# First FFN of a diffusion layer: the up projection by seven block products instead of eight, weight sums by accumulating transfers, hidden tiles through DRAM and the down projection as a phase of its own

## The chip, the core and the metric

The kernel runs on one core of one Trainium2 chip, in one launch. The core has a matrix engine (PE, with its weight loads shown as PEld), a vector engine (DVE), a scalar engine (ACT), GpSimd (POOL) and a queue engine (SP) that issues most DMAs. Times are device microseconds (us) of a whole execution; a version's time is the median of its runs. The profile comes from one execution and names instructions by line of the kernel (L118 is line 118).

## The reference, cut to what matters

One layer (DEPTH = 1) of a diffusion backbone on two sequences of 256 tokens, context and latent, with D = 2048. It begins with a half-step FFN on both sequences, with shared weights; then come a mixer (attention beside an mLSTM), a second FFN on the latent tokens alone and a last norm. All is f32.

```
def half_step_ffn(x, mod, i, g, w_up, w_down):
    h = adaln(x, g, mod, i)
    a, b = jnp.split(h @ w_up, 2, axis=-1)
    return x + 0.5 * mod[:, i + 2, None, :] * ((jax.nn.silu(a) * b) @ w_down)
...
xl = half_step_ffn(xl, mod_l, 0, g_norm[l, 0], w_ffn1_up[l], w_ffn1_down[l])
xc = half_step_ffn(xc, mod_c, 0, g_norm[l, 0], w_ffn1_up[l], w_ffn1_down[l])
```

`mod` has nine rows per sequence: `silu(c) @ w_mod + b_mod` (w_mod is 2048 x 18432). The hidden width D_FF is 5632, 44 columns of 128 (NF), 11 blocks of 512 (FB = 4 columns, CB = 512). `w_up` gives both halves a and b.

## The kernel before

**Products.** Every f32 operand is split into a part that the float32r format holds (`hi`, copied by ACT, L101) and the rest (`lo`, subtracted by DVE, L102). `mm3` (L116) then makes three matmuls, hi x hi, hi x lo, lo x hi (L118 to L120). Activations are split once and stay in SBUF (`hhi`, `hlo`, 512 tokens, context and latent side by side). Weights come from DRAM in tiles of 128 x 2048 f32 (1 MB): `load_split` (L111) issues the load on SP into one of three `raw` buffers, and `split` (L93) makes two halves of 1024 columns, each with its own `hi` and `lo` (four buffers each, so two weight tiles). A tile's halves come free when PE has read them.

**First FFN.** The prologue computes modulation rows 0 and 1 and the norm, and starts the first three columns (NPRE) in six PSUM banks. `ffn` with nt = 4 (L280 on) then goes through the 44 columns: `up` (L302) loads the two halves a and b of a column, with weights stationary and 512 tokens moving: 16 x 3 matmuls each. `tail` (L282) makes silu (L286), gating (L287) and the split of the hidden tile (L298, L299); the tile lies with its columns on partitions, as the down projection needs it. After every fourth column `down` (L367) runs the block before: four column blocks of the output, four token tiles, 4 x 3 matmuls each with 512 weight columns moving, added to `acc` by DVE (L378; the first block is copied by ACT, L376). The last block is `last1` (L508), where the residual, the norm of the next sub-layer and its transposes are woven in. The residual's rows x are added to `acc` by a DMA with accumulation that POOL issues (L506), four in all.

**Modulation rows 2 to 8** are a side job of this FFN: `mod_steps` (L183) loads 224 half tiles of 512 KB (`sraw`, three buffers) and DVE multiplies each with the conditions `cB` and sums (L168, `mod_half`): one product for rows 5 to 8 (latent alone), two for rows 2 to 4, 320 in all. After every `load_split` of the FFN `next(side)` lets a few go; `due` counts products, and MOD_PACE = 3 sets how many.

**Order.** The framework writes each engine's queue: among the instructions whose inputs it takes to be ready, the one earliest in the program goes first, and a buffer's reuse waits for its last reader. `keep_in_program_order` puts an instruction behind the one traced before it on its engine; later ones may still go ahead of it. Each engine then runs its own queue strictly in order.

**Second FFN** (nt = 2): here the weights move (512 columns), tokens are stationary, 24 matmuls for each 1 MB tile; the gated tiles are turned by PE transposes (L359) and copied by ACT (L362).

Of the kernel before, what the change touches and what calls it, by code (L numbers as in the profile page):

```python
# [18 lines left out]
P = 128  # L19
# [11 lines left out]
MOD_PACE = 3.0  # L31
# [17 lines left out]
def tile_layer(ctx: ExitStack, tc: tile.TileContext, I: dict, out: bass.AP):  # L49
# [22 lines left out]
    tri_f = cst.tile([P, P], F32, name="tri_f")  # L72
    tri_b = cst.tile([P, P], F32, name="tri_b")
# [4 lines left out]
    nc.gpsimd.affine_select(out=tri_f, in_=ones, pattern=[[1, P]], compare_op=ALU.is_ge, fill=0.0, base=0, channel_multiplier=-1)  # L78
    nc.gpsimd.affine_select(out=tri_b, in_=ones, pattern=[[-1, P]], compare_op=ALU.is_ge, fill=0.0, base=0, channel_multiplier=1)
    nc.vector.tensor_tensor(ident, tri_f, tri_b, op=ALU.mult)  # L80
# [35 lines left out]
    def mm3(out_ap, sh, sl, mh, ml, first, last):  # L116

        nc.tensor.matmul(out_ap, sh, mh, start=first, stop=False)  # L118
        nc.tensor.matmul(out_ap, sh, ml, start=False, stop=False)  # L119
        nc.tensor.matmul(out_ap, sl, mh, start=False, stop=last)  # L120
# [8 lines left out]
    def sumsq(dst, x, n=512):  # L129
        junk = sm.tile([P, 1024], BF16, tag="junk", name="junk", bufs=1)  # L130
        nc.scalar.activation(junk[:, :n], x, AF.Square, accum_out=dst)
# [25 lines left out]
    mod_rows = {i: dr.tile([2, D], F32, name=f"mod{i}") for i in (2, 5, 8)}  # L157

    cbcm = pool(name="cb", bufs=1)
    cbp = cbcm.__enter__()  # L160
    cB = cbp.tile([P, 2, D], F32, name="cB")
    mT = cbp.tile([P, 9, 2, KT, 2], F32, name="mT")

    def mod_half(raw, i, seqs, kt, h, pinned=False):

        for s in seqs:
            junk = sm.tile([P, 1024], BF16, tag="junk", name="junk", bufs=1)
            ins = nc.vector.scalar_tensor_tensor(  # L168
                junk, raw, 1.0, cB[:, s, h * 1024 : (h + 1) * 1024], op0=ALU.mult, op1=ALU.mult, accum_out=mT[:, i, s, kt, h : h + 1]
            )  # L170
            if pinned:
                tc.keep_in_program_order(ins)
# [10 lines left out]
    def mod_steps(sp):  # L183

        due = 0.0
        for i in range(2, 9):
            seqs = (CTX, LAT) if i < 5 else (LAT,)
            for kt in range(KT):
                for h in range(2):
                    raw = sp.tile([P, 1024], F32, tag="sraw", name="sraw", bufs=3)  # L190
                    nc.sync.dma_start(raw, I["w_mt"][i - 2, kt, :, h * 1024 : (h + 1) * 1024])
                    mod_half(raw, i, seqs, kt, h, True)
                    due += len(seqs)
                    while due > 0:
                        due -= MOD_PACE
                        yield
            for s in seqs:
                n, q = divmod(i, 3)
                if q < 2:
                    dst = (SH, SC)[q][:, n, s, :]  # L200
                    mod_sum(dst, i, s, slice(0, KT))
                    if q:
                        scale_of(n, s, slice(0, KT))
                    continue
                v = sm.tile([P, KT], F32, tag="gv", name="gv")
                mod_sum(v, i, s, slice(0, KT))
                pg = tbank()
                nc.tensor.transpose(pg[:KT, :P], v, ident)
                gr = sm.tile([KT, P], F32, tag="gr", name="gr")
                nc.vector.tensor_copy(gr, pg[:KT, :P])  # L210
                nc.sync.dma_start(mod_rows[i][s, :].rearrange("(k p) -> k p", p=P), gr)
# [5 lines left out]


# [11 lines left out]
    def affine_split(src, n, s, k0, hh, hl):  # L230

        h = sm.tile([P, 2, 256], F32, tag="h", name="h")
# [14 lines left out]
    def drain(it):  # L247
        for _ in it:
            pass
# [29 lines left out]
    def ffn(wup, wdn, hhi, hlo, nt, hp, acc, residual, last, side=iter(()), started=(), row=None):  # L279
        N = nt * P  # L280

        def tail(pab, row=None, dst=None):  # L282
# [14 lines left out]
            hh, hl = dst or [hp.tile([P, N], F32R, tag=g, name=g, bufs=5) for g in ("hidh", "hidl")]  # L297
            nc.scalar.activation(hh, sa, AF.Copy)  # L298
            nc.vector.tensor_tensor(hl, sa, hh.bitcast(F32), op=ALU.subtract)  # L299
            return hh, hl  # L300

        def up(f, dst=None):  # L302
            pab = []
            for ab in range(2):
                wt = load_split(wup[f, ab])
                next(side, None)
# [5 lines left out]
            return tail(pab, None, dst)  # L312
# [54 lines left out]
        def down(n, hids, acc_first, final, between=iter(())):  # L367

            for cb in range(NCB):
                wt = load_split(wdn[n, cb])  # L370
                next(side, None)
# [12 lines left out]
        if nt == 2:  # L384
            hids = []
            for f in range(FB):
                hh, hl = pair() if f % 2 == 0 else (hh, hl)
                dst = hh[:, f % 2, :], hl[:, f % 2, :]
                hids.append(tail(started[f], row, dst) if f < len(started) else up(f, dst))
            for n in range(1, NF // FB):  # L390
                nxt = []
                sab = gated(up_block(n))
                down(n - 1, hids, n == 1, n == NF // FB - 1, turned(sab, nxt))
                hids = nxt
            last(lambda wt, t: block(hids, wt, t))
            return
        hid = {}
        for f in range(NF):
            hid[f] = tail(started[f], row) if f < len(started) else up(f)
            if f % FB == 0 and f:  # L400
                down(f // FB - 1, [hid.pop(q) for q in range(f - FB, f)], f == FB, f // FB == NF // FB - 1)
        hids = [hid.pop(q) for q in range(NF - FB, NF)]
# [8 lines left out]
    hhi = hpool.tile([P, KT, 512], F32R, name="hhi")  # L411
    hlo = hpool.tile([P, KT, 512], F32R, name="hlo")

    pre = [[bank(), bank()] for _ in range(NPRE)]
    with pool(name="st", bufs=1) as st:
        cP = st.tile([P, KT, 32], F32, name="cP")
# [62 lines left out]
    for q in range(2):  # L479
        nc.sync.dma_start(cB[:, q, :], I["cc"][q * KT : (q + 1) * KT, :].rearrange("k p -> (k p)").partition_broadcast(P))  # L480
        nc.scalar.activation(cB[:, q, :], cB[:, q, :], AF.Silu)
# [3 lines left out]
    f1 = f1cm.__enter__()  # L485
    acc = f1.tile([P, 4, D], F32, name="acc", bufs=1)
    ss1 = {}

    def adaln(s):

        for t in range(2):
            x = acc[:, 2 * s + t, :]
            normalised(x, ss1[2 * s + t], s == LAT and t)
        yield
        yield from to_hT([acc[:, 2 * s, :], acc[:, 2 * s + 1, :]], 1, s, hhi, hlo, 256 * s)
# [12 lines left out]
    def last1(block):  # L508
# [3 lines left out]
        for s in (CTX, LAT):  # L512
            for n, cb in enumerate(range(NCB) if s == CTX else reversed(range(NCB))):
                c = slice(cb * CB, (cb + 1) * CB)
                wt = kept.pop(cb, None) or load_split(I["w_dn1"][NF // FB - 1, cb])
# [3 lines left out]
                for t in range(2 * s, 2 * s + 2):  # L519
                    b = block(wt, t)  # L520
# [12 lines left out]
        last1.norm = norm  # L533

    side = mod_steps(f1)
    ffn(I["w_up1"], I["w_dn1"], hhi, hlo, 4, f1, acc, residual1, last1, side, pre)
    drain(side)

# [20 lines left out]
    for s in (CTX, LAT):  # L559
        for g, wt in enumerate(parts):  # L560
            weave(products_of(b_c, wt, 256, range(8 * g, 8 * g + 8), (2 * s, 2 * s + 1)), last1.norm, 1, 0 if g else 4)
        drain(last1.norm)
    f1cm.__exit__(None, None, None)
    cbcm.__exit__(None, None, None)

    with ExitStack() as mx:
        m1 = mx.enter_context(pool(name="m1", bufs=2))
        one = lambda shape, name, dt=F32, tag="": m1.tile(shape, dt, name=name, bufs=1, tag=tag or name)
        gb = one([P, 32], "gb")
# [565 lines left out]
    with pool(name="f2", bufs=2) as f2:  # L1135

# [77 lines left out]
        ffn(I["w_up2"], I["w_dn2"], h2hi[:, :, :T], h2lo[:, :, :T], 2, f2, acc2, residual2, last2, started=pre, row=rB)  # L1214
# [14 lines left out]
def _laid_out(a):  # L1229
# [26 lines left out]
    for n in "12":  # L1256
# [3 lines left out]
        if n == "2":  # L1260

            rest = up[:, :, :, FB:].reshape(4, 4, P, 2, nf // FB - 1, CB)
            m["w_up2b"] = asc(rest.transpose(4, 3, 0, 2, 1, 5).reshape(nf // FB - 1, 2, 4, P, 2048))
            up = up[:, :, :, :FB]
        m[f"w_up{n}"] = asc(up.transpose(3, 2, 1, 0, 4).reshape(-1, 2, P, 2048))
# [35 lines left out]
```

## Time and profile before

| | |
|---|---|
| median of 3 runs | 2812.52 us (2810.99 to 2814.39) |
| the profiled execution | 2813.46 us, its span 2811.7 us |
| mean granted TensorE clock | 0.993 |
| DMA | 525.76 MB, mean 187 GB/s |
| loads of w_up, w_dn, 1 MB each | 4.8 and 4.7 us to landing (median) |
| modulation half tiles, 512 KB | 224, 5.0 us to landing |

The profile has a line for each group of instructions: line, engine, operation, what it writes and reads, count, then busy time and mean duration, then the engine's idle time just before them and what ended it. Matmuls are pipelined, so a matmul's duration is longer than the distance between two. A DMA's "to landing" is from its issue to the arrival of the last byte. Two queues matter: `hardware_dynamic` (issued by SP) and `software_dynamic` (issued by POOL).

### The profile page before, as it was taken

The numbers are of one execution on the slowest core, as the hardware profiler recorded it, in microseconds if no ns is written. First come the engines' busy times: TensorE is split into PE (matmuls) and PEld (weight loads), VectorE is DVE, ScalarE is ACT, GpSimd is POOL, SyncE is SP. The second block draws the span as 40 slices with busy tenths as digits, with TensorE's granted clock in tenths as the row PEclk, the third lists the DMA queues.
The fourth block names the chain that finished last, engine by engine and source line by source line (L and its number), as shares of the span: only waits on it lengthen the run. The fifth ranks groups of instructions, "written<-read, shape, count | busy, mean of one in ns | idle before, by whom it ended". The sixth has DMA issues, their size and how long they took to land. (4 is left out here: it accounts for less than half of the span.)

```text
span 2811.7 us, 32914 instructions
## 1 busy us (share of the span) xinstructions
PE 2766.1 (98%) x13133; PEld 2287.5 (81%) x13133; DVE 1690.4 (60%) x2440; ACT 990.0 (35%) x1287; POOL 53.4 (2%) x83
## 2 busy tenths in 40 slices
PE   6999999999999999999999999999999999999998
PEld 3588888888888888888888988887898888888886
DVE  2366666666666676665437356686684555555557
ACT  3433222222222222222226343545474444444443
POOL 0000000000000000000000000021000000000000
PEclk8999999999999999999999999999999999999999
DMA  8855454544446676764364233435455555555553
GB/s 351 339 190 182 161 187 157 177 168 172 165 166 239 230 252 235 250 236 180 129 186 149 91 119 105 139 127 179 152 195 210 194 194 188 189 193 194 187 189 134
DMA packets 100827, 525.76 MB, mean 187 GB/s; under 512 B 10840, under 2 KB 12856, under 8 KB 55360
## 3 DMA queue, kind: packets, MB, share of 16 engines
q1 hardware_dynamic: 100096, 519.45, 51.9%
q0 software_dynamic: 576, 4.19, 0.7%
q8 instruction: 103, 1.69, 0.2%
q14 instruction: 52, 0.43, 0.0%
HBM read 519.36 MB, written 4.24 MB: 186 GB/s over the span
## 5 line engine op out<-in xcount | busy, mean ns | idle before, releaser
L102 DVE TENSOR_TENSOR lo<-raw,hi 128x1024 fp32r<-128x1024 f32 (+2 forms) x660 | 796.6, 1209 | 750.0 <-ACT hi L101 717.6
L101 ACT ACTIVATE hi<-raw 128x1024 fp32r<-128x1024 f32 (+2 forms) x660 | 688.5, 1046 | 1559.2 <-PE mm L120 714.5
L118 PE MATMUL mm<-hhi,hi 128*128 128x512 f32 (+1 forms) x1664 | 640.1, 385 | 1.2 <-ACT hi L101 1.2
L119 PE MATMUL mm<-hlo,hi 128*128 128x512 f32 (+1 forms) x1664 | 636.6, 383 | 0.0
L120 PE MATMUL mm<-hhi,lo 128*128 128x512 f32 (+1 forms) x1664 | 636.0, 383 | 0.0
L168 DVE SCALAR_TENSOR_TENSOR junk<-sraw,cB 128x1024 bf16<-128x1024 f32 x320 | 391.0, 1222 | 10.4 <-DMA sraw<-in_w_mt 5.2
L118 PEld LDWEIGHTS mm<-hhi,hi 128*128 128x128 f32 x1664 | 313.5, 188 | 68.2 <-issue 5.3
L120 PEld LDWEIGHTS mm<-hhi,lo 128*128 128x128 f32 x1664 | 313.4, 188 | 63.8 <-issue 4.2
L119 PEld LDWEIGHTS mm<-hlo,hi 128*128 128x128 f32 x1664 | 313.4, 188 | 62.6 <-issue 3.3
L118 PE MATMUL mm<-hi,hidh 128*128 128x512 f32 x704 | 274.8, 390 | 0.0
L119 PE MATMUL mm<-lo,hidh 128*128 128x512 f32 x704 | 274.4, 390 | 0.0
L120 PE MATMUL mm<-hi,hidl 128*128 128x512 f32 x704 | 274.2, 390 | 0.0
L118 PE MATMUL mm<-hi,h2hi 128*128 128x512 f32 x640 | 249.3, 390 | 0.0
L120 PE MATMUL mm<-hi,h2lo 128*128 128x512 f32 x640 | 249.3, 389 | 0.0
L119 PE MATMUL mm<-lo,h2hi 128*128 128x512 f32 x640 | 249.3, 389 | 0.0
L378 DVE TENSOR_TENSOR acc<-acc,mm 128x512 f32<-128x512 f32 x216 | 147.8, 685 | 43.5 <-PE mm L120 43.2
L119 PEld LDWEIGHTS mm<-lo,hidh 128*128 128x128 f32 x704 | 132.2, 188 | 27.5 <-DVE lo L102 0.4
L120 PEld LDWEIGHTS mm<-hi,hidl 128*128 128x128 f32 x704 | 132.1, 188 | 27.6 <-DVE hidl L299 0.3
L118 PEld LDWEIGHTS mm<-hi,hidh 128*128 128x128 f32 x704 | 132.2, 188 | 27.3
L118 PE MATMUL mm<-hi,hhi 128*128 128x512 f32 (+3 forms) x384 | 141.3, 368 | 0.0
L119 PEld LDWEIGHTS mm<-lo,h2hi 128*128 128x128 f32 x640 | 120.2, 188 | 24.9
L120 PEld LDWEIGHTS mm<-hi,h2lo 128*128 128x128 f32 x640 | 120.2, 188 | 24.9
(262 smaller groups left out, 2804.4 us busy)
## 6 DMA issues: line engine op xcount, KB each, us to landing
sraw<-in_w_mt SPq DMA_DIRECT2D x224, 512.0 KB, 5.0
raw<-in_w_up SPq DMA_DIRECT2D x91, 1024.0 KB, 4.8
raw<-in_w_dn SPq DMA_DIRECT2D x90, 1024.0 KB, 4.7
raw<-in_w_up2b SPq DMA_DIRECT2D x80, 1024.0 KB, 4.7
mraw<-in_w_m SPq DMA_DIRECT2D x32, 1024.0 KB, 7.1
raw<-in_w_out SPq DMA_DIRECT2D x16, 1024.0 KB, 4.9
gate<-mod SPq DMA_DIRECT2D x32, 256.0 KB, 3.4
raw<-in_w_mk SPq DMA_DIRECT2D x8, 1024.0 KB, 4.9
```

Source lines behind the costliest of these rows:

```text
L101: nc.scalar.activation(hi, src, AF.Copy)
L102: nc.vector.tensor_tensor(lo, src, hi.bitcast(F32), op=ALU.subtract)
L118: nc.tensor.matmul(out_ap, sh, mh, start=first, stop=False)
L119: nc.tensor.matmul(out_ap, sh, ml, start=False, stop=False)
L120: nc.tensor.matmul(out_ap, sl, mh, start=False, stop=last)
L168: ins = nc.vector.scalar_tensor_tensor(junk, raw, 1.0, cB[:, s, h * 1024 : (h + 1) * 1024], op0=ALU.mult, op1=ALU.mult, accum_out=mT[:, i, ...
L378: nc.vector.tensor_tensor(a, a, b, op=ALU.add)
```

## The change

In the first FFN, the three prologue columns and the fourth are computed as before; their gated tiles are written to DRAM (`hidd[0]`). The other ten blocks are computed by `quad`. For one block and one sequence the product is seen as 2 x 2 times 2 x 2: two token tiles by two halves of k (1024 each), times two halves of k by the two column halves a and b (512 columns each). Seven products instead of eight give the four results. Each takes 8 k tiles x 3 matmuls for each sequence, with the weights moving, in two steps q (one 1 MB tile of weights, 24 matmuls).

- **Token side**: the four sums `n1`, `s2`, `s4`, `s3` are made once by DVE and ACT (`token_forms`), the first ahead of the first `quad`, the others in its steps 1 to 6.
- **Weight side**: two tiles `chain_` (one for each q) hold a weight part and become the next sum by a DMA with accumulation issued by POOL, straight after the split of the value before: loaded, then three sums for products 1, 3, 5, 7. `ra` is a `raw` tile loaded for product 4 and summed for product 6. Product 2 uses a plain part. A block thus has 6 plain loads and 8 accumulating ones of 1 MB, and 14 splits instead of 8.
- **Results** are put together in PSUM and by ACT copies and DVE adds (`p1` to `c21`), gated, turned by four PE transposes each (`turned`, one tile a product), copied and written to DRAM (`hidd[n]`).
- **Modulation**: `mod_items` deals half tiles evenly over steps, counted by half tile. 88 of 224 (half h = 0, rows 2 upwards) go to blocks 2 to 10 (126 steps); the other 136 to the down phase (34 steps), those of rows 2 to 4 first. `cB` is loaded again for each phase; in the down phase it and the ring of half tiles lie in the memory of `hlo`. The junk output of the products in the up phase is one of the two `c12` buffers.
- **Down phase**: the ten blocks go in pairs; both blocks of a pair add up in PSUM, so that `acc` is touched once a pair. Hidden tiles of the next pair are loaded and split (`hid_block`) meanwhile. The last block (`last1`) is as before.
- Triangles for the mixer are built later, some scratch tiles move, and `ffn` keeps only the second FFN's form. The file of w_up is laid out in parts (`w_up1b`).

```diff
+        def turned():
+            if not turn:
+                return
+            n, t, ca = turn.pop(0)
+            tb = tbank()
+            for j in range(FB):
+                nc.tensor.transpose(tb[:, j * P : (j + 1) * P], ca[:, j * P : (j + 1) * P], ident)
+            stg = f1u.tile([P, CB], F32, tag="stg", name="stg")
+            nc.scalar.activation(stg, tb, AF.Copy, scale=-1.0)
+            nc.sync.dma_start(hidd[n][:, t].rearrange("p j c -> p (j c)"), stg)
...
+            def p35(s):
+                cb[s] = c12_tile()
+                nc.scalar.activation(cb[s], Y[s], AF.Copy)
+
+            def c12(s):
+                add(cb[s], X[s], cb[s])
+                mul(ca[s], ca[s], cb[s])
+                turn.append((n, 2 * s, ca[s]))
+
+            def c22(s):
+                add(cy[s], X[s], cy[s])
+                ca[s] = ca_tile()
+                nc.scalar.activation(ca[s], X[s], AF.Copy)
+
+            def c21(s):
+                add(ca[s], Y[s], ca[s])
+                nc.scalar.activation(ca[s], ca[s], AF.Silu)
+                mul(ca[s], ca[s], cy[s])
+                turn.append((n, 2 * s + 1, ca[s]))
+
+            accum = lambda dst, src: nc.gpsimd.dma_start(dst, src, accum_op=ALU.add)
+
+            def chained(ab, c):
+                return lambda q: accum(chain_[q], part(n, ab, c + q))
+
+            def again(q):
+                if n + 1 < NB:
+                    first_chain(n + 1, q)
...
+            order = (
+                (a11, held, X, True, chained(1, 0), p1),
+                (a12, plain, Z, True, None, c11),
+                (n1, held, Y, True, chained(1, 2), kept),
+                (s4, loaded, Y, False, lambda q: accum(ra[q], part(n, 1, q)), p35),
+                (s2, held, X, False, chained(0, 2), c12),
+                (s3, lambda q: ra[q], X, False, None, c22),
+                (a22, held, Y, True, again, c21),
+            )
+            for m, (a, src, dst, fresh, then, use) in enumerate(order):
+                if fresh:
+                    dst.update({s: bank() for s in range(2)})
+                for q in range(2):
+                    wt = split(src(q))
+                    if then:
+                        then(q)
+                    after(2 * m + q)
+                    for s in range(2):
+                        for j in range(4):
+                            k = 4 * q + j
+                            hi, lo = a[0][:, s, k, :], a[1][:, s, k, :]
+                            mm3(dst[s], hi, lo, *wt(slice(j * CB, (j + 1) * CB)), fresh and k == 0, k == 7, True)
+                        if q and use:
+                            use(s)
+                        elif not s:
+                            turned()
...
+        side = mod_items(mod_up, sraw, {0: cBh}, lambda: c12_tile().bitcast(BF16), (NB - 2) * 14)
+        for n in range(2, NB):
+            quad(n, lambda step: steps(side))
...
+    spare = hpool.tile([P, KT * 512], F32R, tag="hl", name="spare").bitcast(F32)
+    cBf = spare[:, :4096].rearrange("p (s d) -> p s d", s=2)
+    conditions(cBf, 0, 2)
+    ring = [spare[:, 4096 + 1024 * q : 5120 + 1024 * q] for q in range(4)]
...
+        for cb in range(NCB):
+            bs = [bank() for _ in range(4)]
+            for m in range(2):
+                wt = load_split(I["w_dn1"][p + m, cb])
+                steps(side)
+                steps(ahead)
+                for t in range(4):
+                    block_products(bs[t], p + m, wt, t, m == 0, m == 1)
+                    if m:
+                        a = acc[:, t, cb * CB : (cb + 1) * CB]
+                        if p == 0:
+                            nc.scalar.activation(a, bs[t], AF.Copy)
+                        else:
+                            nc.vector.tensor_tensor(a, a, bs[t], op=ALU.add)
```

More of the change, by code (lines that the diff above doesn't have):

```diff
@@ L129, in sumsq @@
     def sumsq(dst, x, n=512):
[L130 removed]
+        junk = sm.tile([P, 512], BF16, tag="junk", name="junk", bufs=1)
         nc.scalar.activation(junk[:, :n], x, AF.Square, accum_out=dst)
@@ new lines, in mod_items @@
+    def mod_items(items, raws, cB, junk, n_steps):
+        items = list(items)
+        done = 0
+        for n, (i, kt, h) in enumerate(items):
+            while done < n * n_steps // len(items):
+                done += 1
+                yield
+            seqs = (CTX, LAT) if i < 5 else (LAT,)
+            raw = raws()
+            nc.sync.dma_start(raw, I["w_mt"][i - 2, kt, :, h * 1024 : (h + 1) * 1024])
+            mod_half(raw, cB[h], junk, i, seqs, kt, h)
+            left[i] -= 1
+            if not left[i]:
+                mod_end(i, seqs)
@@ L382, in down @@
             drain(between)
[L384 to L402, printed above, removed]
+        hids = []
+        for f in range(FB):
+            hh, hl = pair() if f % 2 == 0 else (hh, hl)
+            dst = hh[:, f % 2, :], hl[:, f % 2, :]
+            if f < len(started):
+                tail(started[f], dst, row)
+            else:
+                up(f, dst)
+            hids.append(dst)
+        for n in range(1, NF // FB):
+            nxt = []
+            sab = gated(up_block(n))
+            down(n - 1, hids, n == 1, n == NF // FB - 1, turned(sab, nxt))
+            hids = nxt
         last(lambda wt, t: block(hids, wt, t))
@@ L484, in tile_layer @@
     f1cm = pool(name="f1", bufs=2)
     f1 = f1cm.__enter__()
+    scratch.append(f1)
     acc = f1.tile([P, 4, D], F32, name="acc", bufs=1)
     ss1 = {}
[L489 to L495, printed above, removed]
+    hid = {}
+    for n in range(2):
+        hid[n] = hid_slot("nt"[n])
+        drain(hid_block(n, *hid[n]))
```

307 lines of the change are left out of this document (228 added, 79 removed).

## The prediction

> **What bounds the kernel now.** I read four views in this order: busy time by engine, fixed stretches, groups of instructions, instructions in order of time.
>
> ```profile
> span 2811.7 us, 32914 instructions
> PE 2766.1 (98%) x13133; PEld 2287.5 (81%) x13133; DVE 1690.4 (60%) x2440; ACT 990.0 (35%) x1287; POOL 53.4 (2%) x83
> ```
>
> ```profile
> 400.00:600.00 200.00, 200.00 (x884) 165.66 (x883) 131.19 (x183) 46.30 (x51) 0.00 (x0) 1.00 0.49 177
> 2200.00:2400.00 200.00, 200.00 (x895) 165.57 (x894) 109.92 (x109) 83.12 (x85) 0.00 (x0) 1.00 0.54 191
> ```
>
> The columns of the stretches are length, busy time with instruction count of PE, PEld, DVE, ACT and POOL, granted clock, DMA share and GB/s. In the first FFN (400 to 600) PE never pauses and starts 884 matmuls in 200 us: 0.2262 us each, although the rows below give each matmul 0.39 us, because they are pipelined. In the second FFN, where the weights are the moving operand as they will be in the new up projection, 895 starts contain about 24 transposes; the pace is the same. So the kernel's time is its number of matmuls times 0.2262 us, and everything else hides: DVE is busy 131 of 200 us, the DMA engines 0.49. A change pays in full for the matmuls that it drops as long as DVE, the DMA engines and the waits between them stay under PE's new, shorter time.
>
> **PE's account.** Before, one block of the first up projection is 2 halves x 4 columns x 16 k x 3 = 384 matmuls. Afterwards it is 7 products x 2 sequences x 8 k x 3 = 336. Ten blocks change, so 480 matmuls go: 480 x 0.2262 = **-108.6 us**. The new form leaves the gated tiles with tokens on partitions, so 16 transposes a block are added. Their price is in the second FFN:
>
> ```profile
> 2229.00 0.39 PE L120 MATMUL mm<-hi,hid2l 128*128 128x512 f32 x1
> 2229.23 0.60 PE L359 MATMUL tr<-ident,sab 128*128 128x128 f32 x4
> 2229.58 0.48 PE L118 MATMUL mm<-hi,hid2h 128*128 128x512 f32 x1
> 2229.90 0.40 PE L119 MATMUL mm<-lo,hid2h 128*128 128x512 f32 x1
> ```
>
> From 2229.00 to 2229.90 there are two matmul intervals and four transposes: (0.90 - 2 x 0.226) / 4 = 0.112 us. 160 of them: **+17.9 us**. The down projection keeps its 192 matmuls a block. PE's own account is -90.7 us. The rest is what this uncovers.
>
> **DVE in the up phase.** The back-to-back pace of each kind of DVE work:
>
> ```profile
> 632.38 0.68 DVE L378 TENSOR_TENSOR acc<-acc,mm 128x512 f32<-128x512 f32 x1
> 632.98 1.22 DVE L102 TENSOR_TENSOR lo<-raw,hi 128x1024 fp32r<-128x1024 f32 x1
> 634.12 1.22 DVE L168 SCALAR_TENSOR_TENSOR junk<-sraw,cB 128x1024 bf16<-128x1024 f32 x1
> 635.26 0.08 DVE L168 DVE_READ_ACCUMULATOR junk<-sraw,cB 128x1 f32 x1
> 635.38 1.22 DVE L168 SCALAR_TENSOR_TENSOR junk<-sraw,cB 128x1024 bf16<-128x1024 f32 x1
> ```
>
> From start to start, an add out of PSUM takes 0.60 us, half a weight split 1.14, one modulation product 1.26. A block's PE time becomes 336 x 0.2262 + 16 x 0.112 = 77.8 us, in 14 steps of 24 matmuls (5.43 us). DVE gets 28 half splits (31.9, against 16 before), 12 adds or gatings (7.2) and modulation: 88 items over nine blocks, of which the first 48 cost two products. That is 19.6 products a block (24.6 us) at first and 12.3 us later. Together 63.7 of 77.8 us (82%), later 51.4 (66%). It fits, but some of it sits in the way: after the fifth product the sixth writes the same two PSUM banks, so DVE's add must come within the other sequence's half step, 2.7 us, and a pair of modulation products (2.5 us) can be in front of it. The adds wait for PE, and splits traced later queue behind them. Also the modulation's junk output borrows the two buffers that hold the fourth product's sum until the fifth is added, so for two steps no modulation product can run and its work is pushed into the other twelve. ACT has 28 half splits and 16 copies or silus:
>
> ```profile
> L101 ACT ACTIVATE hi<-raw 128x1024 fp32r<-128x1024 f32 x626 | 662.9, 1060 | 1520.9 <-PE mm L120 676.9 <-PE mm L119 617.9 <-issue 187.3
> L344 ACT ACTIVATE sab<-mm 128x512 f32<-128x512 f32 x20 | 11.8, 588 | 9.8 <-PE mm L120 9.8
> ```
>
> 28 x 1.06 + 16 x 0.59 = 39 us: half busy, hidden. (Now these splits wait for PE to free buffers; that is the slack that shrinks.)
>
> **The DMA engines in the up phase.** The weight sums are made by accumulating transfers on POOL's queue: 8 a block of 1 MB, beside 6 plain loads of 1 MB, 4.9 MB of modulation weights and 1 MB of gated tiles written. The kernel has just four such transfers (the residual's rows, L506); all ran between 1409 and 1441 us. Three views of that window, DMA queues, issues and stretches:
>
> ```profile
> q0 software_dynamic: 576, 4.19, 63.1%
> q1 hardware_dynamic: 1126, 4.30, 39.1%
> acc<-in_ctx POOLq DMA_DIRECT2D x2, 1024.0 KB, 11.2
> acc<-in_x POOLq DMA_DIRECT2D x2, 1024.0 KB, 16.3
> raw<-in_w_up SPq DMA_DIRECT2D x2, 1024.0 KB, 16.4
> 1409.00:1441.00 32.00, 32.00 (x143) 26.48 (x142) 12.34 (x14) 7.37 (x8) 3.71 (x4) 1.00 1.02 266
> ```
>
> Four transfers took 63.1% of 32 us: 5.05 us of all 16 engines each. The plain queue over the whole span is the row to set beside it:
>
> ```profile
> q1 hardware_dynamic: 100096, 519.45, 51.9%
> ```
>
> 0.519 x 2811.7 / 519.45 = 2.81 us per MB. So a block asks for 8 x 5.05 + 11.9 x 2.81 = 73.8 us of engines in 77.8 us of PE: **95%**, against 49% now. The window shows that a share of 1.02 is reached and PE stays busy (32.00 of 32), but a plain load's landing stretches to 16.4 us. Now the deadline: a chained sum may start when its tile has been split (2.3 us into the step before PE's) and must be there when the split four steps later begins: 4 x 5.43 - 2.3 = 19.4 us, against 11.2 and 16.3 to landing. Six of the eight are issued in six consecutive steps (third to fifth product), and on this queue they go one after another: 6 x 5.05 = 30.3 plus some 5 MB of plain traffic, 14, is 44 us of engine time in 33 us, caught up in the lighter steps after. The first of them moves some 4.5 us after its issue (11.2 to landing less 5.05 of moving leaves 6.2 around it; I put 4.5 before). Counted from that issue, the last is issued at 5 x 5.43 = 27.2 and due at 27.2 + 19.4 = 46.6: at S us each, 4.5 + 6S must stay under 46.6, S under 7.0. In the window, from the first issue to the end of the full share:
>
> ```profile
> 1409.56 1.07 POOL L506 DMA_DIRECT2D acc<-in_ctx  x1 [1377.75 <-DVE acc L499]
> ```
>
> S was (1441 - 1409.6 - 4.5) / 4 = 6.7, with 1.07 MB of plain loads per transfer. That is near: bounds for all waits in the up phase are 0 and some 7 us a block. I take 2 a block for ten blocks, **+20 us**, nearer to zero because the window's PE did not stop.
>
> The Trainium skill, "DMA: Bandwidth & Descriptors", Anatomy of one DMA — SWDGE (gpsimd) path, fits such a transfer as 2.0 us plus bytes over 436e3, an estimate of 4.4 us for 1 MB with 2.4 of it moving. This case's trace has 11.2 to 16.3 to landing and 5.05 of engines, so the row decides here; by that rule the share would be near 68%, and without the 20 us the sum would be 20 lower.
>
> **The down phase.** The 136 remaining modulation items are dealt four to each of 34 steps of 48 matmuls (10.86 us), counted by item and not by product. The first 48 items, the first 12 steps, cost two products each. DVE per step then: eight products 7 x 1.26 + 1.15 = 10.0, one split 2.28, half a hidden tile's split 1.14 in the first four of every eight steps, adds out of PSUM 4 x 0.60 in every second step from the ninth on. That is 13.4, 12.3 and 14.6 us for four steps each: 161 us against PE's 130. DVE is the bound there and PE cannot get it back: **+31 us**. Products come ahead of the next split in program order, so they hold it up. From the thirteenth step DVE has 4 x 1.26 + 2.28 + 0.57 + 1.2 = 9.1 of 10.86, covered. The start costs more: the condition rows land in memory that the last up product frees.
>
> ```profile
> cB<-in_cc SPq DMA_DIRECT2D x2, 1024.0 KB, 14.0
> L481 ACT ACTIVATE cB<-cB x2: 1968/1970/1971, 138.5 to 140.3; 128x2048 f32<-128x2048 f32 x2
> ```
>
> Up to 14.0 + 2 x 1.97 = 18 us pass without a product to do, while PE consumes a step and a half; between 0 and 12 us of DVE time are lost. I take **+6**.
>
> **The seams.** The four token forms cost 28 DVE passes of 1.14 us, 8 of them under the fourth column's up matmuls, 20 in six steps of the first block: 22.8 + 7 x 2.28 = 39 against 38 us of PE, nearly covered. Between the phases, add, silu, gating, transposes, copies and two writes (one buffer) follow the last product, but the down phase starts with blocks 0 and 1, in DRAM long before, so PE need not wait for them. 0 to 12 us for both seams, taken **+6**.
>
> **Sum.** The profiled execution took 2813.5 us (span 2811.7), 0.9 above the median of 2812.5. 2813.5 - 108.6 + 17.9 + 20 + 31 + 6 + 6 = 2785.8; against the median **2785 us**, 1% faster.
>
> **The rivals.**
> A. The sums arrive late (slower). The place is the chained transfers of the fourth and fifth product; it decides at S = 7.0 us, and each 0.1 above costs 6 x 0.1 x 10 = 6 us. At S = 8.1 the waits are 66 instead of 20 us: 2785 + 46 = **2831**. For it: 95% demand and 16.4 us landings under load. Against it: S was 6.7, and a block that stretches lightens its own share.
> B. Products give way to splits in the down phase, because the order on DVE is the scheduler's and their weights land later. Over the whole phase DVE has 184 x 1.26 + 80 x 1.14 + 18 x 1.14 + 80 x 0.6 = 392 of 434 us, so it fits if spread: 2785 - 31 = **2754**.
> C. The pauses cost clock.
>
> ```profile
> 60.00:70.00 10.00, 9.22 (x57) 4.42 (x56) 0.36 (x2) 0.60 (x1) 0.00 (x0) 1.00 0.95 383
> 70.00:80.00 10.00, 7.08 (x40) 3.34 (x44) 6.83 (x14) 7.79 (x14) 0.00 (x0) 0.69 0.94 353
> ```
>
> With 0.8 us idle of 10 the granted clock stayed 1.00, with 2.9 idle it fell to 0.69. The twelve DVE-bound steps leave gaps of 1.5 to 3.8 us. If four to twelve of them lose 0.31 x 10 us, that is 12 to 37 us, so 2797 to 2822, middle **2810**. [...]
>
> **Chances.** Forecast 0.57 (its own range 2758 to 2806, the unknown terms between their ends), A 0.22, B 0.13, C 0.08. The range reaches down past B, where part of the 20 is gone too, and up to most of A: 2742 to 2830. A difference of 0.2%, 5.6 us, is about what a measurement of this kernel can tell from none. Faster: the forecast without its upper edge, and B, 0.67. Same: that edge and part of C, 0.09. Slower: A and the rest of C, 0.24.
>
> **What would show it.** PE should have 13133 - 480 + 160 = 12813 instructions. Software DMA should carry 84 transfers at about 5 us and the DMA share in the up phase be 0.9 to 1.0; if waits of ACT's or DVE's split for the chain tiles lead PE's idle time by more than 3 us a block, A is right. In the first 130 us of the down phase DVE should be busy 95% or more and PE about 80%; PE at 98% there means B. A granted clock under 0.97 there means C. I am wrong altogether if PE's pace per matmul differs from 0.2262 us, or if PE idles at places that no term names.

## The result, and the profile after

The changed kernel takes 2786.07 us (median of 4 runs, 2783.36 to 2787.11), the kernel before 2813.45 in runs on the same chip: a ratio of 0.9902, 95% interval 0.9885 to 0.9919. The forecast was 2785 with the right sign; its terms were not right one by one, which is what the experiments are about.

The first lines of the changed kernel's page, and its two large DMA queues:

```profile
span 2784.2 us, 33137 instructions
PE 2689.2 (97%) x12813; PEld 2216.6 (80%) x12813; DVE 1853.3 (67%) x2565; ACT 1191.7 (43%) x1515; POOL 124.9 (4%) x165
...
q1 hardware_dynamic: 106960, 522.60, 52.2%
q0 software_dynamic: 12096, 88.09, 16.1%
```

PE has the 12813 instructions of the forecast. Of the span it is now idle for 95 us; before it was 46. To see where, I cut the span at events that every version since has: the end of the last transpose of the input rows, the first product of the ten new blocks, the first product of the down phase, its 1921st, and the end of the last products. These are the stretches of the changed kernel; columns as in the prediction (length, busy time and count of PE, PEld, DVE, ACT, POOL, clock, DMA share, GB/s):

```profile
141.15:183.19 42.04, 40.40 (x171) 32.71 (x170) 39.50 (x40) 20.75 (x26) 1.06 (x1) 0.96 0.68 219
183.19:974.37 791.18, 784.81 (x3517) 646.71 (x3516) 576.53 (x682) 387.70 (x444) 69.49 (x79) 1.00 0.94 257
974.37:1440.69 466.32, 439.57 (x1931) 361.72 (x1930) 385.46 (x574) 114.98 (x119) 1.75 (x2) 0.97 0.79 280
1440.69:1500.55 59.86, 50.59 (x217) 40.05 (x216) 41.25 (x57) 28.30 (x56) 3.66 (x6) 0.94 0.76 214
```

A stretch costs its matmuls at 0.22625 us (the 200 us with 884 of the prediction) plus what I call its **loss**. The ten blocks are 3360 matmuls, 760.2 us: a loss of 31.0, of which an undisturbed block explains 21.3: its period is 78.15 us, its 336 matmuls are 76.02, so its 16 transposes cost 0.133 us each. The down phase is 1920 matmuls, 434.4 us: a loss of **31.9**. The last 192 products of the FFN need 43.4: a loss of **16.4**. Before, the same 192 products with the same transposes between took

```profile
1479.56:1527.26 47.70, 46.86 (x217) 38.16 (x216) 39.70 (x55) 28.20 (x57) 1.88 (x4) 1.00 0.51 173
```

so 12.2 us were lost there that no term of the forecast names. The first row, 168 matmuls (the prologue's last 72 and the fourth column's 96), lost 4.0 us, and the last transpose of the input rows has moved from 135.6 to 141.2 us: 5.6 more in the prologue, unnamed too.

Most of what the down phase lost, some 27 us, stands in one place. Four stretches of the changed kernel, then its waits from 1180 to 1240 us, then the instructions of SP's queue:

```profile
1100.00:1120.00 20.00, 20.00 (x90) 16.58 (x89) 19.90 (x31) 3.19 (x3) 0.00 (x0) 1.00 0.69 247
...
1180.00:1200.00 20.00, 16.77 (x72) 12.89 (x70) 16.95 (x27) 2.01 (x2) 0.00 (x0) 1.00 0.85 292
1200.00:1220.00 20.00, 0.00 (x0) 0.00 (x0) 13.56 (x23) 0.52 (x1) 0.00 (x0) 0.52 0.92 314
1220.00:1240.00 20.00, 19.37 (x77) 15.30 (x78) 16.16 (x25) 5.51 (x6) 0.00 (x0) 0.89 0.87 331
```

```profile
ACT hi L102 <- DMA raw<-in_w_dn: 59.0, 4, 34.2
...
PE mm L119 <- ACT hi L102: 23.1, 1, 23.1
```

```profile
1176.40 34.72 SPq L194 DMA_DIRECT2D spare<-in_w_mt  x19
1211.17 0.42 SPq L114 DMA_DIRECT2D raw<-in_w_dn  x1
```

Read them from the bottom. SP issues nineteen modulation loads in a row, each when one of the ring's four slots comes free, and only then the load of w_dn that PE needs next; ACT's split waits 34 us for it, PE 23 us for ACT. In the stretches before, DVE was full (19.90 of 20) and PE lost nothing: the products had fallen behind the splits.

### The profile page after: what moved, and what is told of

It reads as the page before. It is cut to its first block, busy times and chain, and to the rows that moved or that the text cites. A ratio compares the mean times of both kernels' runs of the same rounds, so it can differ in the third digit from the quotient of the medians.

```text
span 2784.2 us, 33137 instructions
## 1 busy us (share of the span) xinstructions
PE 2689.2 (97%) x12813; PEld 2216.6 (80%) x12813; DVE 1853.3 (67%) x2565; ACT 1191.7 (43%) x1515; POOL 124.9 (4%) x165
## 3 DMA queue, kind: packets, MB, share of 16 engines
q0 software_dynamic: 12096, 88.09, 16.1%
## 5 line engine op out<-in xcount | busy, mean ns | idle before, releaser
L103 DVE TENSOR_TENSOR lo<-raw,hi 128x1024 fp32r<-128x1024 f32 (+3 forms) x620 | 745.3, 1207 | 544.4 <-ACT hi L102 510.0
L102 ACT ACTIVATE hi<-raw 128x1024 fp32r<-128x1024 f32 (+3 forms) x620 | 643.8, 1043 | 964.7 <-PE mm L121 727.3
L119 PE MATMUL mm<-hi,hhi 128*128 128x512 f32 (+3 forms) x1024 | 394.0, 385 | 0.0
L120 PE MATMUL mm<-lo,hhi 128*128 128x512 f32 (+3 forms) x1024 | 387.2, 378 | 2.9 <-DVE lo L103 2.9
L121 PE MATMUL mm<-hi,hlo 128*128 128x512 f32 (+3 forms) x1024 | 387.1, 378 | 0.0
L103 DVE TENSOR_TENSOR lo<-chain,hi 128x1024 fp32r<-128x1024 f32 x160 | 194.1, 1223 | 105.1 <-ACT hi L102 103.0
L172 DVE SCALAR_TENSOR_TENSOR mjunk<-spare 128x1024 bf16<-128x1024 f32 x184 | 224.8, 1222 | 16.8 <-DMA spare<-in_w_mt 7.5
L120 PEld LDWEIGHTS mm<-lo,hhi 128*128 128x128 f32 x1024 | 192.7, 188 | 36.1 <-DVE lo L103 5.1
L119 PEld LDWEIGHTS mm<-hi,hhi 128*128 128x128 f32 x1024 | 192.6, 188 | 31.4 <-DVE c L610 0.2
L119 PE MATMUL mm<-hi,hidh 128*128 128x512 f32 x448 | 177.2, 396 | 23.1 <-ACT hi L102 23.1
L172 DVE SCALAR_TENSOR_TENSOR c<-sraw,cBh 128x1024 bf16<-128x1024 f32 x136 | 163.7, 1220 | 15.1 <-DMA sraw<-in_w_mt 14.8
L119 PE MATMUL mm<-hhi,hi 128*128 128x512 f32 (+1 forms) x384 | 141.4, 370 | 2.0 <-ACT hi L102 2.0
## 6 DMA issues: line engine op xcount, KB each, us to landing
chain<-in_w_up1b POOLq DMA_DIRECT2D x60, 1024.0 KB, 11.1
```

The source lines that it names most:

```text
L102: nc.scalar.activation(hi, src, AF.Copy)
L103: nc.vector.tensor_tensor(lo, src, hi.bitcast(F32), op=ALU.subtract)
L119: nc.tensor.matmul(out_ap, sh, mh, start=first, stop=False, skip_group_check=skip)
L120: nc.tensor.matmul(out_ap, sh, ml, start=False, stop=False, skip_group_check=skip)
L121: nc.tensor.matmul(out_ap, sl, mh, start=False, stop=last, skip_group_check=skip)
L172: ins = nc.vector.scalar_tensor_tensor(junk(), raw, 1.0, cB[:, s, :], op0=ALU.mult, op1=ALU.mult, accum_out=mT[:, i, s, kt, h : h + 1])
```

## The experiments

Loss is counted as above. Each kernel is the changed one with the edit shown. The kernel before, measured again beside each of them, had medians of 2813.44 to 2813.75 us, so times of different experiments can be compared.

**1. The down phase's items dealt by product.**

```
-            while done < n * n_steps // len(items):
+            while done < n * n_steps // total:      # n and total count products
```

> The down phase's modulation items are dealt by their number of products (184 products over 34 steps, 5.4 each) and no longer four items to a step. Theory T (the forecast's: steps with eight products ask more of DVE than PE's 10.86 us): every step now asks for 9 to 11.5 us of DVE, the 23.5 us pause at 1197 goes and the kernel is 20 to 30 us shorter than the changed kernel's 2786, so 2756 to 2766. Theory Q (SP's queue: a load of w_dn stands behind a run of modulation loads that each wait for one of four ring slots): the time falls only so far as the runs of modulation loads ahead of a w_dn load get shorter. The longest run falls from 19 to 10 loads, so about half of the pause stays: 10 to 15 us gained, 2771 to 2776.

2781.47 us, ratio to before 0.9886 [0.9869, 0.9902]: 4.6 less than the changed kernel, short of both theories. Its down phase:

```profile
972.79:1433.53 460.74, 443.48 (x1932) 362.27 (x1931) 385.89 (x573) 114.47 (x119) 1.75 (x2) 0.99 0.81 284
```

The loss is still 26.3. The long pause is gone; in its place are nine shorter ones from 1237 to 1366 us. PE's waits from 1220 to 1380 us are 5.9 us for ACT's splits of late w_dn loads, 4.4 for DVE's and 4.8 in one piece for DVE at a transpose of a finished modulation row. So neither the burst of two-product items nor the one long run of loads is the whole cause.

**2. The w_dn loads on POOL's queue.**

```
-                wt = load_split(I["w_dn1"][p + m, cb])
+                wt = load_split(I["w_dn1"][p + m, cb], eng=nc.gpsimd)
```

> The w_dn loads of the down phase are issued from POOL's queue instead of SP's; DVE's work and the dealing by item stay. Theory T (DVE's work is the bound): DVE has the same products to do in the same steps, so the pause only changes its name, to a wait for DVE, and the time stays within 5 us of 2786. Theory Q (the order of SP's queue): no w_dn load waits for a ring slot any more, the pause at 1197 goes, 18 to 25 us gained, 2761 to 2768. A software transfer may hold its bytes longer, which would take some of that back.

2790.83 us, 0.9918 [0.9903, 0.9933], loss 35.0: theory Q's 18 to 25 us are not there, and the time stays within 5 us, as theory T said. With the loads out of the modulation's way, PE stops elsewhere. Waits from 1200 to 1380 us:

```profile
DVE mjunk L172 <- DMA spare<-in_w_mt: 26.1, 18, 4.0
...
PE tr L218 <- DVE gv L178: 15.3, 2, 11.9
```

The transpose of a finished modulation row stands in PE's own queue and waits for DVE, which has not done the row's products yet. The same debt reaches PE by another door, 11.9 us in one piece.

**3. The residual by column blocks.**

```
-        if cb == NCB - 1:
-            nc.gpsimd.dma_start(acc[:, t, :], xsrc[s][tt * P : (tt + 1) * P, :], accum_op=ALU.add)
+        c = slice(cb * CB, (cb + 1) * CB)
+        nc.gpsimd.dma_start(a, xsrc[s][tt * P : (tt + 1) * P, c], accum_op=ALU.add)
```

> The first FFN's residual is added by sixteen accumulating transfers of 256 KB, each straight after its column block, instead of four of 1 MB after a row's last block. If the 16 us lost between 1430 and 1500 come from those four transfers standing straight before the last products (full DMA engines, gates and weights late, the adds of the last tiles waiting for the row): 8 to 14 us gained, 2772 to 2778. If they come from something else there (gate loads behind their modulation rows, DVE's order): within 2 us of 2786.

2773.54 us, 0.9857 [0.9842, 0.9872]: 12.5 less, as expected. In the changed kernel the four transfers are issued from 1434.79 to 1448.82, and DVE then waits for the gates that SP loads:

```profile
1434.79 0.87 POOL L746 DMA_DIRECT2D acc<-in_ctx  x1 [488.81 <-DVE acc L739]
...
1448.82 0.88 POOL L746 DMA_DIRECT2D acc<-in_x  x1 [6.88 <-DVE acc L739]
```

```profile
1453.29 0.69 DVE L739 SCALAR_TENSOR_TENSOR y<-mm,gate 128x512 f32<-128x512 f32 x1 [4.88 <-DMA gate<-mod]
...
1464.22 0.69 DVE L739 SCALAR_TENSOR_TENSOR y<-mm,gate 128x512 f32<-128x512 f32 x1 [5.95 <-DMA gate<-mod]
```

```profile
1455.90 0.50 PE L120 MATMUL mm<-lo,hidh 128*128 128x512 f32 x1 [3.94 <-DVE lo L103]
```

A gate of 5 us in front of DVE's queue holds up the next weight split, and PE waits for that. With the transfers spread out, the last products take

```profile
1440.23:1487.63 47.40, 46.57 (x217) 38.06 (x215) 41.05 (x57) 28.29 (x56) 2.95 (x6) 1.00 0.67 201
```

as long as before the change (47.70).

**4. The weight sums without the addition.**

```
-            accum = lambda dst, src: nc.gpsimd.dma_start(dst, src, accum_op=ALU.add)
+            accum = lambda dst, src: nc.gpsimd.dma_start(dst, src)
```

> The up phase's accumulating transfers become plain transfers of the same bytes on the same POOL queue: the weight sums are left out, each transfer overwrites. The forecast held 20 us of waits for these transfers in the up phase; if that was right, 15 to 20 us are gained, 2766 to 2771. The changed kernel's trace shows about 4 us of gaps in the ten blocks: by that, 2 to 6 us are gained, 2780 to 2784, and the DMA share of the up phase falls from about 1.0 towards 0.8.

2778.05 us, 0.9872 [0.9857, 0.9886]: 8.0 less, about half of what the forecast's 20 us would give and more than the 2 to 6 read off the trace. The ten blocks take 783.07 for 791.18 us, and more than half of that is at their end, where the changed kernel's two gaps around 941 us (2.9 and 1.3 us, with the half clock after them) are gone.

```profile
180.55:963.62 783.07, 781.83 (x3518) 645.80 (x3516) 577.41 (x682) 388.48 (x444) 42.77 (x79) 1.00 0.74 260
```

```profile
chain<-in_w_up1b POOLq DMA_DIRECT2D x60, 1024.0 KB, 5.2
...
q0 software_dynamic: 12096, 88.09, 9.4%
```

The same 84 transfers hold the engines 9.4% of 2773.1 us for 16.1% of 2784.2: 3.1 for 5.3 us each on average (the residual's four still add), landing 5.2 us after issue for 11.1. The DMA share falls from 0.94 to 0.74, and that buys only 8 us.

**5. Forty steps for thirty-four.**

```
-        (NB - 1) * NCB - 6,
+        (NB - 1) * NCB,
```

> The modulation items are dealt, by item as in the change, over all 40 steps of the down phase instead of the first 34 (3.4 items a step for 4). The three down phases measured so far lost 31.9 us (changed kernel), 26.4 (weighed) and 35.0 (POOL's queue) over PE's own time, so neither the dealing nor the queue alone is the cause. Theory W (DVE's sum: 184 products of 1.26 us and the splits and adds of 34 steps are 371 us of DVE in 369 us of PE, so however they are dealt the 34 steps lose what DVE starts late and waits): over 40 steps the sum is 398 of 434, but the first 14 steps still ask 12.0, 10.9 and 13.2 us of DVE, 16 us more than PE has, and the start 6: the loss falls to about 20, 2772 to 2777. Theory Q (the order of SP's queue): the longest run of modulation loads ahead of a w_dn load falls from 19 to 7, so the loss falls to 8 or less, 2760 to 2765.

2762.82 us, 0.9818 [0.9804, 0.9831]: 23.3 less, a time that theory Q gave, and 10 better than W. DVE is asked for more than PE has in the first 14 steps, and PE loses only some 3 us there.

```profile
972.10:1418.53 446.43, 440.03 (x1931) 362.48 (x1930) 384.30 (x574) 115.64 (x119) 1.75 (x2) 0.99 0.83 293
```

The loss is 12.0, between Q's 8 or less and W's 20: only 19.9 of the 23.3 us come in the down phase.

**6. By product, and over forty steps.** The edits of 1 and 5.

> Dealt by number of products and over 40 steps: 4.6 products a step, 9.9 us of DVE and about 10 us of DMA engines in PE's 10.86, the longest run of modulation loads ahead of a w_dn load is 5. Theory W: only the start is lost, 3 to 8 us instead of 31.9, so 2758 to 2764. Theory Q gives the same within 4 us. If a third thing (the ring's four slots, the DMA engines) is the bound, it stays above 2772.

2765.01 us, 0.9826 [0.9812, 0.9839], loss 10.9 in the down phase and 2.6 more in the last products. The even dealing lost little in the first thirty steps (1.7 us) and 9.1 in the last ten: the last modulation loads are issued until 1399 us, and at 1405.7 PE has waited 4.9 us for DVE at the transpose of the last row. Just behind, from 1409.5 on, the residual's four transfers meet the gates, which take 13.9 us to landing, and while PE is at the last products DVE waits

```profile
1427.47 0.69 DVE L739 SCALAR_TENSOR_TENSOR acc<-acc,gate 128x512 f32<-128x512 f32 x1 [7.76 <-DMA gate<-mod]
```

So it is no better than dealing by item, which does more of the products early.

**7. 112 items in the up phase** (`MOD_UP = 112`).

> 112 modulation items instead of 88 are done in the up phase, so 24 of one product each leave the down phase. The up phase's DMA engines are asked for 1.33 MB more a block: 77.5 us in a block of 78.15, 99%. Rival A of the forecast (the sums arrive late): each accumulating transfer takes more than 7.0 us of the queue, up gets 20 to 60 us longer. Theory T/W: up stays within 5 us of 791, because a full share has not stopped PE; in down the first 14 steps still ask 16 us more of DVE than PE has, the rest is light: loss 16 to 22 instead of 31.9, so 2770 to 2778 in all.

2798.55 us, 0.9947 [0.9934, 0.9959]: 12.5 more than the changed kernel. The down phase gained more than W said (loss 6.4 for 16 to 22); the up phase gave back 41.0, a loss of the size that rival A named:

```profile
181.65:1013.81 832.16, 798.16 (x3517) 652.29 (x3516) 601.80 (x730) 386.11 (x444) 69.49 (x79) 0.98 0.93 260
```

```profile
DVE c L172 <- DMA sraw<-in_w_mt: 93.9, 38, 5.4
ACT hi L102 <- DMA chain<-in_w_up1b: 41.7, 14, 7.2
```

In the changed kernel the same two waits are 14.8 and 20.6 us. The landing of the chain transfers went only from 11.1 to 11.4 us; what came late above all are modulation loads, whose products keep their place in DVE's queue ahead of the splits. 24 loads of 524 KB are 12.6 MB; at the 257 GB/s that the changed kernel's up phase moved they would take 49 us, an estimate near the 41 that were lost at 260 GB/s. That the engines give no more is not shown: a stretch of this same phase (659 to 679 us) moved 354 GB/s, and the ring of two half tiles, through which all these loads go, is a rival that no run varies.

**8. Forty steps by product with the residual by columns.** The edits of 1, 3 and 5.

> Weighed dealing over 40 steps together with the residual by column blocks. If the two losses are independent, the gains add: 12.5 from the residual and 22 to 28 from the dealing, so 2746 to 2752. If the sixteen residual transfers now stand beside modulation loads that the 34-step dealing had finished by then, some of it is lost again: up to 2760.

2759.17 us, 0.9807 [0.9794, 0.9821]: the upper end. The last products take 47.41 us, but the down phase loses 17.6, most of it (15.8) in its last ten steps, where PE waits once 4.5 us for DVE's split and once 6.1 us for DVE at the transpose of the last modulation row: residual transfers, gates and the last items share these steps.

**9. Two buffers for h.**

```
-        h = scratch[-1].tile([P, 2, 256], F32, tag="h", name="h")
+        h = scratch[-1].tile([P, 2, 256], F32, tag="h", name="h", bufs=2)
```

> The prologue's scratch tile h of the affine split gets two buffers again; the change moved it from a pool with two into one with one. The prologue's last transpose of the input rows stands at 135.6 us before and at 138.5 to 141.2 in the seven kernels since. If the single buffer is the cause (each split waits for DVE's subtraction of the one before it): 3 to 5.6 us gained, 2780 to 2783, and that transpose back at 136. If the shift is only the clock's phase from run to run: 2786.

2776.29 us, 0.987 [0.9857, 0.9884]: 9.8 less, twice what was expected. The four last transposes of the input rows in the changed kernel and in this one:

```profile
140.83 0.60 PE L238 MATMUL tr<-ident,xs 128*128 128x128 f32 x4
```

```profile
133.14 0.60 PE L238 MATMUL tr<-ident,xs 128*128 128x128 f32 x4
```

7.7 us come in the prologue, where the change had lost 5.6 (the other 2.1 are not explained), and the 168 matmuls after it take 38.50 us for 42.04. DVE at the second and third of four pairs of k, in the changed kernel and in this one:

```profile
76.01 0.54 DVE L250 TENSOR_SCALAR h<-tr,SC,SH 128x256 f32<-128x256 f32 x1 [1.55 <-ACT hhi L248]
...
79.27 0.54 DVE L250 TENSOR_SCALAR h<-tr,SC,SH 128x256 f32<-128x256 f32 x1 [1.99 <-ACT hhi L248]
```

```profile
74.12 0.54 DVE L250 TENSOR_SCALAR h<-tr,SC,SH 128x256 f32<-128x256 f32 x1
...
75.56 0.54 DVE L250 TENSOR_SCALAR h<-tr,SC,SH 128x256 f32<-128x256 f32 x1 [0.17 <-ACT hhi L248]
```

One buffer makes ACT, DVE and PE take turns: these four pairs start 2.4 to 3.3 us apart for 1.4.

**10. Fewer second products, everything else kept.**

```
-            seqs = (CTX, LAT) if i < 5 else (LAT,)
+            seqs = (CTX, LAT) if i < 5 - 2 * h else (LAT,)
```

> 32 of the down phase's second products (rows 3 and 4) are left out, with their part of the condition; items, loads and the 34 steps stay. DVE's sum over the 34 steps falls from 371 to 331 of PE's 369 us. Theory W (DVE's sum is what makes the loss, the place varies): the debt of the first steps is repaid in the lighter ones before it shows, the loss falls from 31.9 to 8 or less: 2758 to 2764. Theory Q (only the order of SP's queue): the longest runs of modulation loads ahead of a w_dn load are 13 and 9, so 10 to 17 us of loss stay: 2766 to 2773.

2762.50 us, 0.9822 [0.9809, 0.9836], loss 10.7. The time is theory W's; the loss is above W's 8 and at the low end of Q's 10 to 17. It has runs of 13 and 9 modulation loads ahead of a w_dn load, where the changed kernel has one of 19, so the order of SP's queue moved with DVE's work; PE's longest wait in the down phase, 3.2 us for ACT's split, follows these runs.

```profile
972.32:1417.46 445.14, 439.49 (x1931) 362.41 (x1930) 349.97 (x505) 114.91 (x119) 1.74 (x2) 0.99 0.83 294
```

**11. Forty steps by item, residual by columns, two h.** The edits of 3, 5 and 9.

> Items dealt by item over forty steps, the residual by column blocks, h in two buffers. If the three gains are independent: 2786 less 23.3, 12.5 and 3 to 5.6, so 2745 to 2748. If the sixteen residual transfers meet the modulation loads that forty steps leave at the end: 2750 to 2756.

**2742.98 us** (2741.17 to 2746.52), 0.9751 [0.9737, 0.9764], 43 less than the changed kernel; the three gains singly are 23.3, 12.5 and 9.8, together 45.6. It is a little under the expected 2745 because the two h gave more than was put down for them.

```profile
span 2740.9 us, 33162 instructions
PE 2681.2 (98%) x12813; PEld 2215.0 (81%) x12813; DVE 1852.4 (68%) x2565; ACT 1191.8 (43%) x1515; POOL 135.3 (5%) x177
```

What it still loses: 29.9 us in the ten blocks (21.3 of it transposes) and 12.4 in the down phase.

**What made the loss of the down phase.** By the time, Q came out right in experiment 5 and W in experiment 10; by the loss of the down phase, which is what they are about, neither did by itself. Q alone is ruled out by experiment 2, where no w_dn load waits behind a modulation load and the loss stays. W's figure for experiment 5 was wrong because it charged each overloaded step at once. Set beside DVE's work over all the steps with items, the figures agree. Counted again by the prediction's durations, the 34 steps with items ask 184 x 1.26 + 34 x 2.28 + 18 x 1.14 + 52 adds and 4 gatings of 0.60 = 363 us of DVE in 369 of PE, 98%; the expectation of experiment 5 had counted too many adds (371). Forty steps ask 391 of 434, 90%; experiment 7 333 of 369, 90%; experiment 10 323 of 369, 88%.

| | DVE's share of the steps with items | loss, us |
|---|---|---|
| changed kernel; 1; 2; 3; 4; 9 | 98% | 31.9; 26.3; 35.0; 34.3; 31.7; 35.1 |
| 5; 6; 7; 8; 11 | 90% | 12.0; 10.9; 6.4; 17.6; 12.4 |
| 10 | 88% | 10.7 |

Experiments 3, 4 and 9 leave the dealing and DVE's share in the down phase as they are, 11 deals as 5 does and 8 as 6, so these show the scatter; the different cases are few. The loss goes with DVE's share; the dealing, the queue and the residual's transfers move it by some 10 us and decide where it shows. My reading, argued from the table and not followed step by step: a debt of DVE costs nothing while products may fall behind; it falls due when they must be done, at a ring slot that SP waits for or a transpose in PE's queue. With 2% of slack it cannot be repaid before that, with 10% most of it is. That 98% cost 26 to 35 us and not less is not worked out from rows; the ring's round trip (in experiment 2 DVE itself waits 26.1 us for items) is a likely part, but no run has a larger ring.

## Why the prediction came out right, point by point

The profiled execution went from 2813.46 to 2785.93 us, -27.5. From the losses above: -108.6 for 480 matmuls, + 83.3 of loss (4.0 + 31.0 + 31.9 + 16.4), less 7.0 that the kernel before lost in the same stretch (1391.65 us for 6120 matmuls), + 5.6 in the prologue = -26.7; the other 0.8 are behind the FFN. Against the forecast's terms:

- **PE's own account** held: 480 matmuls at the same pace. A transpose costs 0.133 us and not 0.112: 21.3 for 17.9.
- **The waits of the up phase, +20**, are a term that was mis-sized: 9.7 (31.0 less 21.3), and experiment 4 gives 8.0 for all that the additions cost. Demand was right (0.94 for 95%), DVE too (576.53 of 791 us, 73%). The choice of 2 us a block was wrong: a full DMA share delays transfers that still have time. The Trainium skill's fit for a software transfer ("DMA: Bandwidth & Descriptors", Anatomy of one DMA — SWDGE (gpsimd) path), by which 1 MB is estimated at 4.4 us, is near what experiment 4 shows without the addition (5.2 to landing) and far from the 11.1 of the changed kernel, whose transfers add.
- **Rival A** did not happen, but it was close: experiment 7 with 1.33 MB more a block lost 41 us, inside A's price. Its mechanism was only in part A's: modulation loads came late more than sums (DVE's waits for them rose by 79 us, ACT's for the sums by 21). Whether the engines or the ring held the loads back stays open.
- **The down phase, +31 and +6**: 31.9 in all. The cause, DVE's work against PE's, was right; the way and the place were not, and that the size agrees is luck. The forecast said that products hold up the splits of their own step, so that the first twelve steps lose 31 us, and that PE would be at 80% in the first 130 us:

```profile
974.37:1104.37 130.00, 127.11 (x565) 104.80 (x564) 120.42 (x183) 45.82 (x52) 0.00 (x0) 1.00 0.86 300
```

  PE is at 98%, and the twelve steps lost 4.0 us; some 27 came from 1197 us on. Experiment 1 takes away the burst from which the 31 were worked out, and 26.3 stay. The start cost PE less than 1 us, although the first product ran only at 986.6, 12.2 us into the phase. PE at 98% was to mean **rival B**. B's mechanism came, products behind splits, but not B's 31 us: it holds that a debt fits if spread, and 34 steps at 98% leave little room to repay it. B priced the whole phase (392 of 434) where the items had only 34 of its 40 steps; experiment 5, which gives them all forty, gains 19.9 of B's 31 in this phase.
- **Rival C** did not come: the granted clock in the first 130 us was 1.00 and there were no twelve gaps. Where the clock fell after a pause elsewhere, its cost is part of the losses above.
- **The seams, +6**: 4.0 at the first, nearly all of it the single h (0.5 is left in experiment 9); the second is within the 9.7.
- **Unnamed**: the residual's transfers straight before the last products (12.2 us, 12.5 in experiment 3), because the forecast followed the moved work and not what came to stand next to it; and the buffer count of a scratch tile that moved to another pool (9.8 in experiment 9). PE idle at places that no term names was the forecast's own sign of being wrong.

So PE's account was foreseen, but the closeness of the total is luck: 10 us too much in the up phase, 5 too much in the down phase and 2 at the seams met 18 of unnamed loss; the dearer transposes (3.4) met 2.7 that the kernel before had lost elsewhere in that stretch and the 0.8 behind the FFN.

## What to carry to other kernels

An engine can run a debt for hundreds of microseconds without PE noticing; ask by when it must be repaid and whether the steps until then have slack, and price a queue that is shared with the lagging work as the place where it falls due. When a phase moves, look at what now stands side by side, and at every tile whose pool changed: two such side effects cost 22 us here, where all the costs that the forecast priced came to 81. A DMA share of 0.94 with PE almost never idle can be near the edge: for one more change, work out the MB that it would add and divide them by the GB/s that the stretch moves. Here that estimate was 49 us for 41 measured.

## What the runs showed of the hardware

- An accumulating transfer of 1 MB holds the DMA engines 5.3 us and lands after 11.1 (changed kernel); the same bytes on the same queue without the addition 3.1 (a mean in which the residual's four still add) and 5.2 us (experiment 4).
- In the changed kernel's trace PE's granted clock is 1.00 or 0.50, nothing between; other figures in the rows are means over a stretch. After a wait of 2.49 us at 941 us and one of 0.77 us just behind it, it was 0.50 for some 3.4 us, from 944.7 to 948.1; after a single wait of 2.89 us at 1039 it stayed 1.00. In the pause of 23.1 us it fell 3 us in, at 1200.7, and was low until 1224.6, 4 us after PE had started again. The kernel before lost clock between 70 and 80 us (0.69 in the prediction's row) with no single wait over 1.89 us. So the length of one pause alone did not decide it. These rows contain the first two:

```profile
935.00:955.00 20.00, 16.73 (x67) 13.01 (x66) 12.88 (x16) 8.05 (x9) 0.88 (x1) 0.91 0.85 204
1036.00:1046.00 10.00, 7.11 (x33) 5.56 (x33) 9.93 (x21) 3.20 (x4) 0.00 (x0) 1.00 0.86 294
```
